# Half as many, twice as wide: preparing a projection's weights in 16 halves, and another order of banks at two stage changes of a hybrid gMLP and SSD layer

## The chip, the cores and the metric

One Trainium2 chip, one NeuronCore of it. The metric is the device time of one execution in microseconds, taken as the median of several runs. TensorE (PE) does the matmuls, VectorE (DVE), ScalarE (ACT) and GpSimd (POOL) the elementwise work, and SyncE (SP) and ScalarE issue the DMAs. [...]

## The reference

One layer of a hybrid decoder on a sequence of 1024 rows of width 1024, all float32. The lines that matter here:

```
proj = h @ w_in                                   # 11296 columns in 8 parts
y_a = spatial_gating(gelu(gm_u), gelu(gm_v), ...) * silu(gm_z)
y_b = ssd_scan(...) + xh * d_skip                 # 2048 columns
y_b = rms_norm((y_b * silu(ssm_z)) in 8 groups, ssm_norm_w)
merged = sigmoid(g_a) * (y_a @ w_proj_a) + sigmoid(g_b) * (y_b @ w_proj_b)
out = rms_norm(x + gate * (merged @ w_out), final_norm_w)
```

`h` is the normalised and modulated input; `w_proj_b` has 2048 rows and 1024 columns.

## The kernel before

**Products.** Every large product is done with a rounded high part and a remainder: an operand `t` is copied to `hi` by ScalarE (which rounds it) and VectorE computes `lo = t - hi`; the product is then the three terms hi x hi, hi x lo and lo x hi, added up in a PSUM bank of 128 x 512. The larger products are also done by a seven-product scheme of block matrices (`p1` to `p7`), which needs sums and differences of the four blocks of each operand.

**Stages in order.** Normalisation and modulation with the first gate columns (pool `ps0` of PSUM); the V block (`v_block`, lines 815 to 936), which multiplies by the V columns of `w_in`; then pairs of 128-column blocks of `w_in` (`pair`, line 536 issues the matmuls, 12 for one product, seven products for a pair); then the SSD scan, with `y_a @ w_proj_a` filled in between (`proj_a`); then `y_b @ w_proj_b`, called the second projection here (`multiply`, line 1552); then `merged @ w_out` and the last normalisation.

**Order of work.** Matmuls and all loads are pinned to program order, and with them a few copies. The other instructions of an engine are ordered by a planner ahead of time, which takes those first whose data it expects to be ready and whose place in the program is earlier. What an engine has in its list is then fixed: a copy or a store that must wait holds up all behind it on its engine. `later(d, f, ...)` puts the call `f` behind the d-th product from now; `run_tasks` is called once for each product, so a delay counts products.

**The second projection's weights.** From pair 16 on, while TensorE works on the pairs of `w_in`, the kernel forms the planes of `w_proj_b` that the seven products need and writes them to the DRAM tensors `wb_d`. A quarter `(k, j)` is 128 columns of each of four blocks: `wb_load` reads it in two DMAs on SyncE into the raw tile `wbr` (two buffers). Then `wb_parts` copies a plane to its high part on ScalarE (line 791), and one product later `wb_low` computes the remainder on VectorE (line 796) and stores both parts through ScalarE's queue. This is done for one plane (`wba`), and after the four sums on VectorE in `wb_sums` (lines 808 to 811) for two planes each in `wbb` and `wbc`. Each of the three tags has one buffer. There are 32 quarters, one for each 4.3 products; `wb_quarter` loads the next one as it begins.

**The start of the V block.** Its first four banks `vx0` to `vx3` are taken from pool `ps1`, which lies over `ps0`. The last two of `ps0`'s four accumulators are still read by the tanh of the first gate (`first_gate`, line 473, tile `sg`) when the block begins. Unit `u` is one (product, k), of 12 matmuls; units 0 and 1 run term by term over all four banks, later units bank by bank.

**The start of the second projection.** `banks` takes tiles of pool `ps3`, which lies over `ps1`, and a tag gets its bank when it is first named: `y0`, `y1`, `y2`, then `x0` to `x3`, then `y3`. p1 accumulates in the x banks. The y banks serve in p1 for four small results: `pq6_1` and `pq7_1` behind units 1 and 2, `pr6` and `pr7` behind units 3 and 4 (`rows_bank`). The last product of `proj_a` leaves two halves (`pma`) that VectorE multiplies with the gate (line 1382, tile `tha`); in the program as laid out before, they are in banks 5 and 0, and VectorE's part of them is pinned behind the operands of the first four units of p1.

Of the kernel before, what the change touches and what calls it, by code (L numbers as in the profile page):

```python
# [8 lines left out]
F32 = mybir.dt.float32  # L9
# [26 lines left out]
def hybrid_kernel(  # L36
# [739 lines left out]


    WB = {"p5": 0, "p7": 1, "p6": 2, "p3": 3, "p4": 4}
    quarters = [(k, j) for k in range(KT) for j in range(4)]
    wbr = {}  # L780

    def wb_load(i):

        k, j = quarters[i]
        wbr[i] = raw = pre.tile([P, 4, P], F32, name=f"wbr{i}", tag="wbr", bufs=2)
        for k0, t in ((k, raw[:, 0:4:3]), (k + KT, raw[:, 1:3])):
            load(t, w_proj_b[k0 * P : (k0 + 1) * P, :].rearrange("p (b j c) -> p j b c", b=2, j=4)[:, j])

    def wb_parts(i, name, at, n, t):
        hl = pre.tile([P, n, 2, P], F32R, name=f"{name}{i}", tag=name)  # L790
        A.copy(hl[:, :, 0], t)
        later(1, wb_low, i, hl, at, n, t)

    def wb_low(i, hl, at, n, t):
        k, j = quarters[i]
        V.tensor_sub(hl[:, :, 1], t, f32(hl[:, :, 0]))
        store(wb_d[k][:, at : at + n, :, j * P : (j + 1) * P], f32(hl))

    def wb_quarter(i):
        if i + 1 < len(quarters):  # L800
            wb_load(i + 1)
        wb_parts(i, "wba", 4, 1, wbr[i][:, 2:3])
        later(1, wb_sums, i)

    def wb_sums(i):
        raw = wbr.pop(i)
        a11, a12, a22, a21 = (raw[:, n] for n in range(4))
        V.tensor_add(a22, a22, a21)
        V.tensor_sub(a21, a11, a21)
        V.tensor_sub(a11, a22, a11)  # L810
        V.tensor_sub(a12, a12, a11)
        wb_parts(i, "wbb", 0, 2, raw[:, 2:4])
        wb_parts(i, "wbc", 2, 2, raw[:, 0:2])

    def v_block():

        V_OPS = (("p1", "b11", "x"), ("p5", "t1", "y"), ("p6", "t2", "x"), ("p3", "b22", "y"), ("p7", "t3", "x"),
                 ("p2", "b21", "y"), ("p4", "t4", "x"))
        units = [(nm, k) for nm, _, _ in V_OPS for k in range(4)]
        kept, wops, pair_of = {}, {}, {}  # L820
        early = 6

        def quadrant(nm, k):

            r, c = {"11": (0, 0), "21": (0, 1), "22": (4, 1), "12": (4, 0)}[nm]
            w = wt(f"av{nm}_{k}", "ws", 8, F32)
            load(w, w_in[(r + k) * P : (r + k + 1) * P, COL_V + c * 512 : COL_V + (c + 1) * 512])
            return w

        def loads(u):  # L830
            nm, k = units[u]
            live[0] += 2 if nm in ("p5", "p7") else 1
            pair_of[u] = [quadrant(q, k) for q in {"p1": ("11",), "p5": ("21", "22"), "p6": ("11",), "p3": ("12",),
                                                    "p7": ("11", "21"), "p2": ("12",), "p4": ("22",)}[nm]]

        def operands(u):
            nm, k = units[u]
            q = pair_of.pop(u)
            keep = pin if u < early else lambda i: i
            t = q[-1]  # L840
            if nm == "p5":
                keep(V.tensor_add(t, q[0], t))
                kept[k] = t
            elif nm == "p6":
                t = kept[k]
                keep(V.tensor_sub(t, t, q[0]))
            elif nm == "p3":
                t = kept.pop(k)
                keep(V.tensor_sub(t, q[0], t))
            elif nm == "p7":  # L850
                keep(V.tensor_sub(t, q[0], t))
            hi, lo = wt(f"{nm}v{k}h", "wh", 8), wt(f"{nm}v{k}l", "wl", 8)
            keep(A.copy(hi, t))
            keep(V.tensor_sub(lo, t, f32(hi)))
            wops[u] = hi, lo
            live[0] -= {"p1": 1, "p5": 1, "p6": 1, "p3": 2, "p7": 2, "p2": 1, "p4": 1}[nm]
            ahead()

        live, loaded = [0], [0]

        def ahead():
            while loaded[0] < len(units) and live[0] + (2 if units[loaded[0]][0] in ("p5", "p7") else 1) <= 8:
                loads(loaded[0])
                loaded[0] += 1

        LEAD = 3
        ahead()
        operands(0)
        operands(1)
        first_dt()  # L870
        first_gate(0)
        first_gate(1)
        open_banks()
        ps = {"x": [psum.tile([P, 512], F32, name=f"vx{j}", tag="px", bufs=2) for j in range(2)]}
        ps["x"] += [bank(f"vx{j}") for j in (2, 3)]
        res = {}

        def result(nm):
            res[nm] = [wide(f"v{nm}{i}") for i in range(2)]

        def part(nm, j):
            return res[nm][j // 2][:, j % 2 * 512 : (j % 2 + 1) * 512]

        def finished(nm, i):

            rows, c = (0, 4)[nm[2] == "2"] + 2 * i, (0, 1)[nm[1] == "2"]
            w = res[nm][i]
            A.activation(w, w, AF.Gelu_apprx_tanh)
            for j in range(2):
                V.bn_stats(bst[:, rows + j, c, :], w[:, j * 512 : (j + 1) * 512])  # L890
                store(v_d[4 * c : 4 * c + 4].rearrange("g p q -> p g q")[:, :, (rows + j) * P : (rows + j + 1) * P],
                      w[:, j * 512 : (j + 1) * 512].rearrange("p (g q) -> p g q", g=4))

        def emptied(nm):
            with tc.high_priority():
                for j in range(4):
                    b = ps["x" if nm in ("p1", "p6", "p7", "p4") else "y"][j]
                    if nm in ("p1", "p5", "p6", "p4"):
                        to = {"p1": "c11", "p5": "c22", "p6": "c12", "p4": "c21"}[nm]
                        if j == 0:  # L900
                            result(to)
                        A.copy(part(to, j), b)
                    else:
                        to = {"p3": "c12", "p7": "c22", "p2": "c11"}[nm]
                        V.tensor_add(part(to, j), part(to, j), b)
            if nm in ("p3", "p7", "p2", "p4"):
                for i in range(2):
                    later(1 + i, finished, to, i)

        for u, (nm, k) in enumerate(units):  # L910
            _, bn, pn = V_OPS[u // 4]
            if u == 4:
                ps["y"] = [bank(f"vy{j}") for j in range(4)]
            (bh, bl), (wh, wl) = (bop[bn][v][k] for v in range(2)), wops[u]
            terms = list(enumerate(((bh, wh), (bl, wh), (bh, wl))))
            for j, (n, (l, r)) in [(j, t) for t in terms for j in range(4)] if u < 2 else [(j, t) for j in range(4) for t in terms]:
                js = slice(j * P, (j + 1) * P)
                pin(PE.matmul(ps[pn][j], l[:, js], r, start=nm in ("p1", "p5", "p2") and n + k == 0,  # L918
                              stop=n == 2 and k == 3, skip_group_check=nm not in ("p1", "p5", "p2")))
            wops.pop(u)  # L920
            if u == 0:
                operands(2)
                last_split("t2")
            elif u == 1:
                operands(3)
                last_split("t3")
            elif u == 2:
                last_split("t4")
                operands(4)
            if u > 1 and u + LEAD < len(units):  # L930
                operands(u + LEAD)
            if k == 3:
                emptied(nm)
                if nm == "p3":
                    ps["y"] = [bank(f"vz{j}") for j in range(4)]
            run_tasks()
# [382 lines left out]
    for n, (name, _, _, d1, d2, g) in enumerate(todo):  # L1319
        if n == 0:  # L1320
            later(5, stats)
        if n == NPRE:
# [1 line left out]
            prepool = tc.tile_pool(name="prepool", bufs=1, side="right", reuse_waits="tile")  # L1324
            pre = prepool.__enter__()
            wb_load(0)
            for i in range(len(quarters)):
                later(2 + 43 * i // 10, wb_quarter, i)
        if n == len(jobs):
            while tasks:  # L1330
                run_tasks()
# [108 lines left out]
    room.extend(tag for k in range(KT - 2) for tag in ya_tags[k])  # L1440
    draw(left[0] - 5)

    def banks(name, c, n=4):
        return [psb.tile([P, 512], F32, name=f"{name}{j}", tag=f"b{c}{j}") for j in range(n)]

    big_r = [0]

# [218 lines left out]
    for u, (nm, k) in enumerate(units):  # L1666
        if k == 0:
            if nm == "p1":
                psy = banks("yp3", "y", 3)
                psx = banks("x", "x")  # L1670
                psy += [psb.tile([P, 512], F32, name="yp33", tag="by3")]
                rows_bank[0] = lambda name: psy[("pq6_1", "pq7_1", "pr6", "pr7").index(name)]
            elif nm in ("p5", "p2"):
                psy = banks(f"y{nm}", "y")
            ps = psy if nm in ("p2", "p5", "p3") else psx
# [206 lines left out]
```

## Time and profile before

| | us |
|---|---|
| median of 3 runs | 1404.81 (1404.6 to 1406.76) |
| the profiled execution | 1402.83 |
| its span, first to last instruction | 1401.1 |
| PE busy | 1369.7 |
| DVE busy | 1055.3 |
| ACT busy | 804.7 |
| POOL busy | 217.8 |

The mean granted clock of TensorE is 0.996. In a row of the timeline the columns are the start in us from the beginning of the span, the duration in us, the engine, the line of the kernel, the operation, `out<-in` by the program's tile names, shapes, count, and in brackets how long the engine had stood still before it and what ended that. ACTq and SPq are the DMA issues of ScalarE and SyncE. In a row for a tile stand the shortest, median and longest duration in ns and the first and last start. A row of waits has the time in total, the number of times and the longest.

### The profile page before, as it was taken

Reading aid. Unit: us, or ns where it says so; the run is one execution under the profiler, and the core shown is the slowest. Engines: PE = TensorE matmul, PEld = TensorE weight load, DVE = VectorE, ACT = ScalarE, POOL = GpSimd, SP = SyncE. Lnnn points to the kernel's source line nnn. Section 1 sums busy time; section 2 is a strip of 40 time slices with the busy share of each in tenths; the row PEclk is TensorE's granted clock in tenths of the full one; section 3 lists DMA queues with packets and bytes.
Section 4 is the critical chain, followed back from the end, with each engine's and each line's share of the span. In section 5 each row is a group of like instructions: output and inputs, shape, how many; then the busy total and the mean of one; then the engine's idle time right before and its main releaser. Section 6 shows DMA issues by size and latency. Waiting matters only on the chain.

```text
span 1401.1 us, 20579 instructions
## 1 busy us (share of the span) xinstructions
PE 1369.7 (98%) x6971; PEld 1135.3 (81%) x6971; DVE 1055.3 (75%) x1815; ACT 804.7 (57%) x1496; POOL 217.8 (16%) x208
## 2 busy tenths in 40 slices
PE   8999999999999999999999999999999999999997
PEld 7678888888888888878888888888888788888786
DVE  4776776687777889888888795398777655859976
ACT  5754656666666566455675555677676623223453
POOL 0000000000000011211000110038878750000001
PEclk9999999999999999999999999999999999999999
DMA  8775433333434777777775774598887658878913
GB/s 263 197 237 147 120 121 120 105 123 118 135 105 128 225 219 230 220 238 226 215 220 148 241 214 134 179 354 319 279 267 278 220 185 280 319 254 313 378 44 120
DMA packets 277181, 288.62 MB, mean 206 GB/s; under 512 B 15788, under 2 KB 224084, under 8 KB 277076
## 3 DMA queue, kind: packets, MB, share of 16 engines
q1 hardware_dynamic: 182420, 203.76, 45.6%
q10 hardware_dynamic: 94656, 83.54, 18.1%
q8 instruction: 55, 0.90, 0.3%
q14 instruction: 50, 0.41, 0.1%
HBM read 199.79 MB, written 87.46 MB: 205 GB/s over the span
## 4 chain that ended last, share of the span: by engine, by line
PE 78%; DVE 7%; DMA 7%; ACT 3%; issue 3%; POOL 2%; SPq 1%; ACTq 0%; DVEq 0%; POOLq 0%
PE xuz L536 6%; PE xx L536 6%; PE xcb L536 6%; PE xz L536 5%; PE xg L536 5%; PE pma L81 4%; PE yx L536 3%; PE vx L918 3%; PE x L1552 3%; PE yuz L536 3%; PE yp L1552 3%; PE ycb L536 3%; PE yz L536 3%; PE ox L1745 2%; PE yg L536 2%
## 5 line engine op out<-in xcount | busy, mean ns | idle before, releaser
L759 POOL TENSOR_TENSOR wog<-wog,gb 128x256 f32<-128x256 f32 x16 | 21.5, 1362 | 624.0 <-DMA wog<-in_w_out_dram 602.9
L1075 ACT ACTIVATE dcy<-dcy,nacs 128x128 f32<-128x128 f32 x256 | 78.7, 388 | 17.2 <-POOL dcy L1070 16.1
L1070 POOL TENSOR_SCALAR_AFFINE_SELECT dcy<-dcy 128x1024 f32<-128x1024 f32 x32 | 35.0, 1094 | 135.4 <-DMA yl<-ya_d 88.7
L990 ACT ACTIVATE ac<-ac 128x1024 f32<-128x1024 f32 x32 | 33.9, 1060 | 25.8 <-DVE ac L988 22.6
L1067 ACT ACTIVATE ea<-dcy 64x512 f32<-64x512 f32 x64 | 40.0, 626 | 12.2 <-DMA dcy<-acs_d 11.8
L81 PE MATMUL pma<-yh,wah 128*128 128x512 f32 x128 | 43.8, 423 | 0.0
L81 PE MATMUL pma<-yh,wal 128*128 128x512 f32 x128 | 43.2, 419 | 0.0
L1490 DVE SCALAR_TENSOR_TENSOR yn<-yn,par,rb 128x512 f32<-128x512 f32 x32 | 23.9, 747 | 24.8 <-DMA yn<-yb_d 24.8
L1155 DVE TENSOR_TENSOR ym<-yn,ea 128x512 f32<-128x512 f32 (+1 forms) x32 | 19.9, 622 | 29.9 <-PE yn L81 29.7
L1095 DVE TENSOR_TENSOR dcy<-dcy,pc 128x1024 f32<-128x1024 f32 x32 | 38.9, 1217 | 3.8 <-PE pc L84 2.6
L1157 POOL TENSOR_TENSOR yz<-y,sl 128x512 f32<-128x512 f32 x32 | 41.4, 1294 | 1.1
L81 PE MATMUL pma<-yl,wah 128*128 128x512 f32 x128 | 40.3, 396 | 0.0
L1156 POOL TENSOR_TENSOR y<-y,ym 128x512 f32<-128x512 f32 (+1 forms) x32 | 36.6, 1143 | 14.5 <-DVE ym L1155 14.5
L81 PE MATMUL yi<-dcy,xd 128*64 128x128 f32 x512 | 35.9, 284 | 2.9 <-DVE st L1125 2.9
L81 PEld LDWEIGHTS yn<-sl,st 128*128 128x128 f32 x224 | 30.3, 190 | 8.8 <-issue 2.7
L81 PE MATMUL yn<-sl,st 128*128 128x128 f32 x224 | 31.4, 276 | 5.4 <-DVE st L1125 5.4
L81 PE MATMUL sp<-xe,bn 128*128 128x256 f32 x112 | 33.6, 418 | 2.9 <-DVE ssq L1186 1.7
L988 DVE SCALAR_TENSOR_TENSOR ac<-c2x,cwt,ac 128x1023 f32<-128x1023 f32 (+2 forms) x24 | 31.2, 1298 | 5.7 <-ACT ac L986 5.6
L1760 POOL TENSOR_TENSOR r<-r,fnw 128x512 f32<-128x512 f32 x2 | 2.5, 1296 | 208.2 <-ACT junk L1758 208.2
L988 DVE SCALAR_TENSOR_TENSOR ac<-c2cb,cwt,ac 128x1023 f32<-128x1023 f32 (+2 forms) x24 | 31.1, 1294 | 4.8 <-ACT ac L986 4.7
L1123 POOL TENSOR_TENSOR st<-st,cd 128x256 f32<-128x256 f32 x48 | 32.5, 677 | 11.2 <-PE yn L81 7.1
L952 ACT ACTIVATE vm<-vm,vr 128x128 f32<-128x128 f32 x64 | 25.8, 483 | 14.0 <-DMA vm<-v_d 13.5
(2903 smaller groups left out, 4421.7 us busy)
## 6 DMA issues: line engine op xcount, KB each, us to landing
sl<-s_d SPq DMA_DIRECT2D x32, 768.0 KB
s_d<-ac ACTq DMA_DIRECT2D x32, 512.0 KB
dcy<-acs_d SPq DMA_DIRECT2D x32, 512.0 KB
av<-in_w_in_dram SPq DMA_DIRECT2D x36, 256.0 KB
aw<-in_ada_w_dram SPq DMA_DIRECT2D x16, 512.0 KB
wbr<-in_w_proj_b_dram SPq DMA_DIRECT2D x64, 128.0 KB
wb_d<-wbb ACTq DMA_DIRECT2D x32, 256.0 KB
wb_d<-wbc ACTq DMA_DIRECT2D x32, 256.0 KB
```

The lines of the kernel that those rows point to most:

```text
L81: pin(PE.matmul(acc, l, r, start=first, stop=last))
L536: pin(PE.matmul(ps, lw[:, k * P : (k + 1) * P], r[k], start=first and n + k == 0, stop=n == 2 and k == 3, skip_group_check=not first))
L918: pin(PE.matmul(ps[pn][j], l[:, js], r, start=nm in ("p1", "p5", "p2") and n + k == 0, stop=n == 2 and k == 3, skip_group_check=nm not in ...
L988: V.scalar_tensor_tensor(ac[:, s:], cc[:, : S - s], conv_wt[:, 3 - s, i : i + 1], ac[:, s:], op0=ALU.mult, op1=ALU.add)
L990: A.activation(ac, ac, AF.Silu)
L1067: A.activation(ea[hh * HD : (hh + 1) * HD], dcy.rearrange("p (j e) i l -> p e j (i l)", e=2)[hh * HD : (hh + 1) * HD, hh], AF.Exp)
L1070: G.affine_select(out=d8, in_=d8, compare_op=ALU.is_ge, fill=-1e30, base=0, pattern=[[0, 2 * HPG], [1, P]], channel_multiplier=-1)
L1075: A.activation(dcy[:, h, i, :], dcy[:, h, i, :], AF.Exp, bias=sub[:, i, h : h + 1])
L1095: V.tensor_tensor(d3, d3, pc[:, 0:256].unsqueeze(1).to_broadcast([P, HPG, 256]), op=ALU.mult)
L1156: G.tensor_add(y1[:, :, t0:], y1[:, :, t0:], m[:, :, t0:])
L1157: G.tensor_mul(yz, y1, sl[:, 4:6])
L1552: pin(PE.matmul(ps[j], a[:, v, js], r, start=first and n + k == 0, stop=n == 2 and k == KT - 1, skip_group_check=not first))
```

## The change

Three edits in one diff.

1. `w_proj_b` is prepared in 16 halves of 256 columns, one for each 8.6 products. The raw tile `wbr` has one buffer; its load is issued two products ahead of the half's first copy, no longer by the half before. `wbb` and `wbc` become one tag, `wbb`, of one buffer, and the second pair of planes is copied three products after the first.
2. The first two units of the V block start with two of their three terms on the first two banks only; the third and fourth banks come after that.
3. The eight banks of pool `ps3` are named in an order written out by hand: `y2, y0, x0, x1, x2, y3, x3, y1`.

```
--- before.py
+++ after.py
@@ -776,29 +776,27 @@
 
 
     WB = {"p5": 0, "p7": 1, "p6": 2, "p3": 3, "p4": 4}
-    quarters = [(k, j) for k in range(KT) for j in range(4)]
+    halves_b = [(k, j) for k in range(KT) for j in range(2)]
     wbr = {}
 
     def wb_load(i):
 
-        k, j = quarters[i]
-        wbr[i] = raw = pre.tile([P, 4, P], F32, name=f"wbr{i}", tag="wbr", bufs=2)
+        k, j = halves_b[i]
+        wbr[i] = raw = pre.tile([P, 4, 2 * P], F32, name=f"wbr{i}", tag="wbr")
         for k0, t in ((k, raw[:, 0:4:3]), (k + KT, raw[:, 1:3])):
-            load(t, w_proj_b[k0 * P : (k0 + 1) * P, :].rearrange("p (b j c) -> p j b c", b=2, j=4)[:, j])
+            load(t, w_proj_b[k0 * P : (k0 + 1) * P, :].rearrange("p (b j c) -> p j b c", b=2, j=2)[:, j])
 
     def wb_parts(i, name, at, n, t):
-        hl = pre.tile([P, n, 2, P], F32R, name=f"{name}{i}", tag=name)
+        hl = pre.tile([P, n, 2, 2 * P], F32R, name=f"{name}{at}_{i}", tag=name)
         A.copy(hl[:, :, 0], t)
         later(1, wb_low, i, hl, at, n, t)
 
     def wb_low(i, hl, at, n, t):
-        k, j = quarters[i]
+        k, j = halves_b[i]
         V.tensor_sub(hl[:, :, 1], t, f32(hl[:, :, 0]))
-        store(wb_d[k][:, at : at + n, :, j * P : (j + 1) * P], f32(hl))
+        store(wb_d[k][:, at : at + n, :, j * 2 * P : (j + 1) * 2 * P], f32(hl))
 
     def wb_quarter(i):
-        if i + 1 < len(quarters):
-            wb_load(i + 1)
         wb_parts(i, "wba", 4, 1, wbr[i][:, 2:3])
         later(1, wb_sums, i)
 
@@ -810,7 +808,7 @@
         V.tensor_sub(a11, a22, a11)
         V.tensor_sub(a12, a12, a11)
         wb_parts(i, "wbb", 0, 2, raw[:, 2:4])
-        wb_parts(i, "wbc", 2, 2, raw[:, 0:2])
+        later(3, wb_parts, i, "wbb", 2, 2, raw[:, 0:2])
 
     def v_block():
 
@@ -911,13 +909,19 @@
             _, bn, pn = V_OPS[u // 4]
             if u == 4:
                 ps["y"] = [bank(f"vy{j}") for j in range(4)]
-            (bh, bl), (wh, wl) = (bop[bn][v][k] for v in range(2)), wops[u]
-            terms = list(enumerate(((bh, wh), (bl, wh), (bh, wl))))
-            for j, (n, (l, r)) in [(j, t) for t in terms for j in range(4)] if u < 2 else [(j, t) for j in range(4) for t in terms]:
-                js = slice(j * P, (j + 1) * P)
-                pin(PE.matmul(ps[pn][j], l[:, js], r, start=nm in ("p1", "p5", "p2") and n + k == 0,
+            at = [(u, n, j) for j in range(4) for n in range(3)]
+            if u == 0:
+                ends = [(0, 2, 0), (0, 2, 1)] + [(0, n, j) for j in (2, 3) for n in range(3)]
+                at = [(i, n, j) for i in range(2) for n in range(2) for j in range(2)] + ends
+            elif u == 1:
+                at = [(1, 2, 0), (1, 2, 1)] + [(1, n, j) for j in (2, 3) for n in range(3)]
+            for i, n, j in at:
+                (bh, bl), (wh, wl) = (bop[bn][v][units[i][1]] for v in range(2)), wops[i]
+                l, r = ((bh, wh), (bl, wh), (bh, wl))[n]
+                pin(PE.matmul(ps[pn][j], l[:, j * P : (j + 1) * P], r, start=nm in ("p1", "p5", "p2") and n + units[i][1] == 0,
                               stop=n == 2 and k == 3, skip_group_check=nm not in ("p1", "p5", "p2")))
-            wops.pop(u)
+            if u:
+                wops.pop(u)
             if u == 0:
                 operands(2)
                 last_split("t2")
@@ -1324,8 +1328,10 @@
             prepool = tc.tile_pool(name="prepool", bufs=1, side="right", reuse_waits="tile")
             pre = prepool.__enter__()
             wb_load(0)
-            for i in range(len(quarters)):
-                later(2 + 43 * i // 10, wb_quarter, i)
+            for i in range(len(halves_b)):
+                if i:
+                    later(43 * i // 5, wb_load, i)
+                later(2 + 43 * i // 5, wb_quarter, i)
         if n == len(jobs):
             while tasks:
                 run_tasks()
@@ -1440,8 +1446,8 @@
     room.extend(tag for k in range(KT - 2) for tag in ya_tags[k])
     draw(left[0] - 5)
 
-    def banks(name, c, n=4):
-        return [psb.tile([P, 512], F32, name=f"{name}{j}", tag=f"b{c}{j}") for j in range(n)]
+    def banks(name, c):
+        return [psb.tile([P, 512], F32, name=f"{name}{j}", tag=f"b{c}{j}") for j in range(4)]
 
     big_r = [0]
 
@@ -1666,9 +1672,8 @@
     for u, (nm, k) in enumerate(units):
         if k == 0:
             if nm == "p1":
-                psy = banks("yp3", "y", 3)
-                psx = banks("x", "x")
-                psy += [psb.tile([P, 512], F32, name="yp33", tag="by3")]
+                first = {t: psb.tile([P, 512], F32, name=f"{t}p", tag=f"b{t}") for t in ('y2', 'y0', 'x0', 'x1', 'x2', 'y3', 'x3', 'y1')}
+                psx, psy = ([first[f"{v}{j}"] for j in range(4)] for v in "xy")
                 rows_bank[0] = lambda name: psy[("pq6_1", "pq7_1", "pr6", "pr7").index(name)]
             elif nm in ("p5", "p2"):
                 psy = banks(f"y{nm}", "y")
```

## The prediction

> **What bounds the kernel now.** I read the page first, then who waited for whom on TensorE, then the stretches around each wait in order of time.
>
> ```profile
> span 1401.1 us, 20579 instructions
> ...
> PE 1369.7 (98%) x6971; PEld 1135.3 (81%) x6971; DVE 1055.3 (75%) x1815; ACT 804.7 (57%) x1496; POOL 217.8 (16%) x208
> ```
>
> TensorE is busy for 98% of the span, so nothing that is only made cheaper on VectorE, ScalarE or the DMA queues shortens the run. Time can come only from the places where TensorE stands still. The waits of TensorE name them (in total, times, longest):
>
> ```profile
> PE vx L918 <- ACT sg L473: 1.3, 1, 1.3
> ...
> PE xz L536 <- ACT c2z L552: 1.2, 2, 0.7
> PE xg L536 <- ACT c2g L552: 1.1, 2, 0.7
> PE x L1552 <- DVE tha L1382: 1.0, 1, 1.0
> ```
>
> These four rows are what the change touches: the start of the V block (vx), the stretch in which the second projection's weights are prepared (xz, xg), and the start of the second projection (x). They add to 4.6 us of a span of 1401.1 us. The profiled execution took 1402.83 us, 1.73 us more than its span, and the median of the runs is 1404.81 us. I make the sum on the span and take the same difference off the median. A difference of 0.2%, or 2.8 us, is about what can be told from none here.
>
> **Transition one, the V block.** The chain that ended last gives TensorE's pace where nothing holds it: 48 matmuls of 512 columns in 10.88 us, so 0.2267 us each.
>
> ```profile
> 83.13 10.88 PE vy L918 x48
> ```
>
> Around the start of the block, first TensorE, then VectorE, then ScalarE (start, duration):
>
> ```profile
> 70.46 0.85 PE L918 MATMUL vx<-p1v0h,b11h 128*128 128x512 f32 x3
> 72.61 0.50 PE L918 MATMUL vx<-p1v0h,b11h 128*128 128x512 f32 x1 [1.30 <-ACT sg L473]
> 72.94 0.40 PE L918 MATMUL vx<-p1v0h,b11l 128*128 128x512 f32 x1
> ```
>
> ```profile
> 71.50 0.69 DVE L854 TENSOR_TENSOR p1v0l<-av,p1v0h 128x512 fp32r<-128x512 f32 x1
> 72.11 0.69 DVE L854 TENSOR_TENSOR p1v1l<-av,p1v1h 128x512 fp32r<-128x512 f32 x1
> ```
>
> ```profile
> 71.94 0.62 ACT L473 ACTIVATE sg<-acc 128x512 f32<-128x512 f32 x1
> ```
>
> The fourth matmul opens the fourth bank, and that bank still holds the last quarter of the first gate, which the tanh reads until 71.94 + 0.62 = 72.56. Without the wait the fifth matmul would start at 70.46 + 4 x 0.2267 = 71.37; it starts at 72.94. The loss is 1.57 us.
>
> The new order gives TensorE eight matmuls on the first two banks (two of three terms of units 0 and 1), then the third term of unit 0 there, and only then the third and fourth banks. The third bank is opened by matmul 11 (72.73) and the fourth by matmul 14, at 70.46 + 13 x 0.2267 = 73.41, 0.85 us after the tanh has ended. The order needs two operands earlier. p1v0l is first read by matmul 9, at 72.27, and is ready at 71.50 + 0.69 = 72.19. This is the next late thing, with a margin of 0.08 us; one VectorE instruction more ahead of it would give back about 0.6 us. p1v1l (ready 72.80) is read by matmul 17, at 74.09. No matmul is added, and the list of waits has no other row of the V block, so the operands behind these keep ahead of TensorE today. Bounds: 0.9 to 1.57 us saved; I take 1.57, because the rows place every operand ahead of its use. TensorE has full queues afterwards, so the whole block and what follows move up.
>
> **Transition two, proj_a to the second projection.** TensorE, then VectorE:
>
> ```profile
> 1156.42 0.39 PE L1552 MATMUL x<-p1bh,p1a 128*128 128x512 f32 x1
> ...
> 1158.93 0.50 PE L1552 MATMUL x<-p1bh,p1a 128*128 128x512 f32 x1 [0.99 <-DVE tha L1382]
> 1159.27 0.40 PE L1552 MATMUL x<-p1bl,p1a 128*128 128x512 f32 x1
> ...
> 1163.14 1.06 PE L81 MATMUL yp<-ones,sq 128*128 128x1 f32 x9
> ```
>
> ```profile
> 1156.93 0.69 DVE L1533 TENSOR_TENSOR p1a<-p1r,p1a 128x512 fp32r<-128x512 f32 x1
> ...
> 1158.20 1.28 DVE L1382 SCALAR_TENSOR_TENSOR tha<-tha,pma 128x512 f32<-128x512 f32 x2
> ```
>
> Six matmuls run on x0 and x1; the seventh opens x2, whose bank still holds half of the last product of proj_a. VectorE empties the two halves only from 1158.20, behind the operands of unit 3. The eighth matmul would start at 1156.42 + 7 x 0.2267 = 1158.01 and starts at 1159.27: 1.26 us lost. Banks are given in the order in which the code first names their tags. Before, x0 to x3 are banks 3 to 6; in the program as it is laid out the two halves lie in banks 5 and 0. After, bank 0 is y2, bank 5 is y3, and x0 to x3 are banks 2, 3, 4 and 6. y2 and y3 are first needed for the row transposes pr6 and pr7, behind units 3 and 4 of p1 and so after the yp row at 1163.14; the halves are emptied by 1158.20 + 1.28 = 1159.48. So the wait goes, with nothing late behind it: unit 3's operands end at 1157.62 and are needed at 1156.42 + 36 x 0.2267 = 1164.58. Bounds 0 (the halves lie elsewhere after the change) to 1.26; I take 1.26.
>
> Does this reach the end? The last stretch has VectorE full:
>
> ```profile
> 1230.00:1240.00 10.00, 10.00 (x46) 8.29 (x45) 2.77 (x4) 2.40 (x4) 0.00 (x0) 1.00 0.80 258
> 1300.00:1340.00 40.00, 38.66 (x170) 31.53 (x169) 40.00 (x67) 21.41 (x39) 0.00 (x0) 1.00 0.89 334
> ```
>
> ```profile
> 1328.78 0.50 PE L1745 MATMUL oy<-wlt,ma11h 128*128 128x512 f32 x1 [1.34 <-DVE wlt L1632]
> ```
>
> (The columns are stretch, length, then busy time of PE, PEld, DVE, ACT and POOL, clock, DMA share, GB/s.) From 1300 VectorE is busy all the time and TensorE waits 1.34 us for it. But between 1230 and 1240 VectorE is busy only 2.77 of 10 us, so it keeps step with TensorE there, and what it starts later moves with TensorE. I count the 1.26 us in full.
>
> **The weights.** In this stage, for all work and then for the instructions that touch the raw tile (DVE, ACT):
>
> ```profile
> 437.00:832.00 395.00, 392.69 (x1740) 323.32 (x1739) 335.56 (x623) 237.04 (x410) 34.97 (x24) 1.00 0.72 215
> ```
>
> ```profile
> 437.00:832.00 395.00, 75.68 (x224) 34.99 (x96) 1.00 0.72 215
> ```
>
> ```profile
> L808 DVE TENSOR_TENSOR wbr<-wbr x32: 276/282/833, 456.3 to 825.0; 128x128 f32<-128x128 f32 x32
> ...
> L791 ACT CAST wbb<-wbr x32: 389/406/410, 457.3 to 826.4; 128x256 fp32r<-128x256 f32 x32
> ...
> L796 DVE TENSOR_TENSOR wbb<-wbr,wbb x32: 406/416/426, 458.1 to 827.5; 128x256 fp32r<-128x256 f32 x32
> ```
>
> A doubled width costs VectorE 0.416 in place of 0.282 us (rows L808 and L796), and 512 columns 0.69 (the p1v0l row). A half then costs 5 x 0.416 + 2 x 0.69 = 3.46 us on VectorE, 55.4 us for 16, where 75.68 are spent now: 20 us less. ScalarE: 0.406 + 2 x 0.62 (the tanh row has that width) = 1.65 us, 26.3 us for 16 in place of 34.99. 64 loads become 32, 96 stores 48, with the same bytes. All of this lies beside TensorE, so by itself it is worth nothing. What counts is TensorE's loss in the stage: 395.00 - 392.69 = 2.31 us, the four waits for c2z and c2g. One of them, ScalarE then TensorE:
>
> ```profile
> 779.50 0.30 ACT L791 CAST wba<-wbr 128x128 fp32r<-128x128 f32 x1 [3.88 <-DMA wbr<-in_w_proj_b_dram]
> ...
> 785.32 0.59 ACT L552 COPY c2g<-xg 128x512 f32<-128x512 f32 x1 [0.91 <-DVE wbb L796]
> ```
>
> ```profile
> 785.96 1.20 PE L536 MATMUL xg<-t4h,p4g10h 128*128 128x512 f32 x4 [0.46 <-ACT c2g L552]
> ```
>
> ScalarE stood 3.88 us for the load of the raw tile, later 0.91 us because the store of wbb is queued in front of the copy and waits for VectorE; the copy that empties TensorE's bank was then late. Over the stage this wait for the load is the largest of ScalarE:
>
> ```profile
> ACT wba L791 <- DMA wbr<-in_w_proj_b_dram: 27.0, 15, 4.2
> ```
>
> What the change does to it has two sides. For: half as many loads, copies and stores to stand behind, and 20 us less in VectorE's queue. Against: the load is now issued two products ahead of its copy (2 x 12 x 0.2267 = 5.4 us) in place of 4.3 (11.7 us); it carries twice the bytes; and on SyncE it waits until the last reader of the one raw tile is through, with the w_in loads of the next pairs queued behind it. The last reader is issued five products after the half begins, the next load 1.6 products (4.4 us) later, so that wait should mostly be over. The second pair of planes shares the buffer of the first, so its copy on ScalarE waits for that store, issued two products earlier; behind it stand the copies that empty the banks. Best case: all four waits go, 2.31 us saved. Worst case: a wait like these four, 2.31 / 4 = 0.58 us, at each of 16 halves, 16 x 0.58 - 2.31 = 7.0 us lost. I take half of the best case, 1.2 us saved, because the stage of before is the nearest row and the work in front of the copies falls.
>
> [...]
>
> Sum: 1.57 + 1.26 + 1.2 = 4.0 us. Span 1397.1, profiled execution 1398.8, median 1400.8 us.
>
> **Rivals.**
> - All goes well: the four waits vanish too, 1.57 + 1.26 + 2.31 = 5.1 us, 1399.7 us. For it: 20 us less on VectorE. Against: the shorter lead. Chance 0.13.
> - The transitions gain and the weights cost: the load waits reach TensorE as often as now or a little more, by up to 2.8 us. 1402 to 1404.8, middle 1403. Chance 0.13.
> - The change does not do what it says at transition two: the rotating banks of proj_a are given out as they come free, and a changed order may put a half of the last product under x0 to x3 again. 1.57 + 1.2 = 2.8 us, 1402.0 us. Against: nothing near that place is changed. Chance 0.07.
> - Slower, the single raw tile: each half makes ScalarE stand for its load. TensorE feels it when the copy is more than 5.44 - 0.59 = 4.85 us late (two products less the copy). The longest wait now is 4.2 us; a lead that is 6.3 us shorter can carry it past that at every half. The stage then loses 16 times x in place of 2.31 us, against 2.83 us from the transitions. At x = 0.5 us that is 8.0 - 2.31 - 2.83 = +2.9, 1407.7 us; at 0.8 us 12.8 - 5.14 = +7.7, 1412.5 us. From 0.5 us per half it decides. For it: 15 of 32 copies wait already. Against: the planner orders ScalarE's work by when it expects the data, so the copy is likely put later. The four waits of now are 0.5 to 0.7 us each, so I price it near the lower end, 1408 us. Chance 0.22.
>
> **How the numbers follow.** Forecast 0.45, rivals 0.13, 0.13, 0.07, 0.22. Faster by over 0.2% are the forecast and the good case, 0.58; within 0.2% the second and third rivals, 0.20; slower 0.22. The forecast's own range is 1399.7 to 1402.0. The range for 8 in 10 runs from 1398.0, where VectorE's relief helps elsewhere too, to 1407.5, short of the slow rival's middle.
>
> **What would show it.** Right: no wait of vx on sg, none of x on tha, unit 2 of the V block 1.5 us earlier, TensorE's loss in the weights' stage at 1 to 2 us, VectorE's work on the raw tile near 55 us. Wrong: waits of xz, xg, xcb or xx on ScalarE's copies that add to more than 5 us, with wba or the second wbb copy standing ahead of them; or a wait of x on tha.

## The result and the profile after

The changed kernel takes 1400.2 us (median of 10 runs, 1398.12 to 1403.9), the kernel before 1406.29 us (10 runs beside it, 1404.22 to 1410.73). The ratio is 0.9958 with a 95% interval of 0.9942 to 0.9973: 5.9 us less (3.8 to 8.2). The forecast was 1400.8 us and 4.0 us less. It stood on a before of 1404.81 us, so the gains are compared here, not the times.

The profiled executions are no fair pair. The one of before took 1402.83 us, below every one of the 10 runs beside the change; the one of after took 1403.9 us, the slowest of its 10. So the spans (1401.1 and 1402.1 us) say nothing of the gain; I compare stretches between the same two matmuls instead. The head of the page of after:

```profile
span 1402.1 us, 20253 instructions
...
PE 1374.4 (98%) x6971; PEld 1139.7 (81%) x6971; DVE 1045.4 (75%) x1703; ACT 802.2 (57%) x1448; POOL 220.0 (16%) x208
```

VectorE has lost 112 instructions and 9.9 us, ScalarE 48 instructions and 2.5 us. The waits of TensorE in after (total, times, longest):

```profile
PE xx L536 <- ACT c2x L552: 2.0, 1, 2.0
PE xuz L536 <- ACT c1uz L552: 1.8, 1, 1.8
...
PE y3p L84 <- POOL ssq L1194: 0.3, 1, 0.3
...
PE oy L1750 <- DVE wlt L1638: 0.2, 1, 0.2
```

The rows of vx on sg, of x on tha and the four small ones of xz and xg are gone. A longer one of xx, one of y3p on GpSimd, and a longer one of xuz (0.27 us in before) are new.

**V block**, TensorE and then VectorE of after:

```profile
72.06 0.62 PE L921 MATMUL vx<-p1v0h,b11h 128*128 128x512 f32 x2
72.52 0.62 PE L921 MATMUL vx<-p1v0h,b11l 128*128 128x512 f32 x2
72.97 0.62 PE L921 MATMUL vx<-p1v1h,b11h 128*128 128x512 f32 x2
73.43 0.62 PE L921 MATMUL vx<-p1v1h,b11l 128*128 128x512 f32 x2
73.88 0.69 PE L921 MATMUL vx<-p1v0l,b11h 128*128 128x512 f32 x2
```

```profile
73.10 0.69 DVE L852 TENSOR_TENSOR p1v0l<-av,p1v0h 128x512 fp32r<-128x512 f32 x1
```

Eight matmuls run on two banks, and the ninth starts at 73.88, 0.09 us after its operand (73.10 + 0.69 = 73.79); the prediction had a margin of 0.08.

**Second projection**, the first matmul of p1, VectorE's part of the two halves, then the row transposes with GpSimd's power in front of the second:

```profile
1159.51 0.39 PE L1558 MATMUL x0p<-p1bh,p1a 128*128 128x512 f32 x1
...
1174.09 0.27 PE L84 MATMUL y2p<-ident,ssq 128*8 128x128 f32 x1
...
1177.40 0.27 PE L84 MATMUL y3p<-ident,ssq 128*8 128x128 f32 x1 [0.28 <-POOL ssq L1194]
```

```profile
1161.82 1.28 DVE L1388 SCALAR_TENSOR_TENSOR tha<-tha,pma 128x512 f32<-128x512 f32 x2
```

```profile
1175.71 1.64 POOL L1194 TENSOR_TENSOR ssq<-ssq,nhalf 128x8 f32<-128x8 f32 x1 [5.22 <-DVE ssq L1190]
```

TensorE no longer waits for the halves, which VectorE empties until 1163.10. It comes to the second transpose earlier, and the power ends only at 1175.71 + 1.64 = 1177.35.

**The weights' stage**: the stretch 437 to 832 of after for all work, the same for the instructions on the raw tile (DVE, ACT), then ScalarE's waits in it:

```profile
437.00:832.00 395.00, 392.95 (x1739) 324.57 (x1739) 325.62 (x512) 233.80 (x362) 36.34 (x24) 1.00 0.68 212
```

```profile
437.00:832.00 395.00, 57.97 (x111) 25.68 (x47) 1.00 0.68 212
```

```profile
ACT wba L791 <- DMA wbr<-in_w_proj_b_dram: 24.3, 11, 4.7
ACT wbb L791 <- DMA wb_d<-wbb: 23.9, 14, 3.0
```

VectorE does the raw tile in 57.97 us in place of 75.68, ScalarE in 25.68 in place of 34.99. The wait for the load is about as large as before (27.0), and beside it stands a new one: the second pair of planes waits for the store of the first, nearly every time. TensorE stood 2.05 us, in one wait:

```profile
646.23 0.41 ACT L791 CAST wba<-wbr 128x256 fp32r<-128x256 f32 x1 [4.66 <-DMA wbr<-in_w_proj_b_dram]
...
649.00 1.24 ACT L990 ACTIVATE ac<-c1x,par,cwt 128x1024 f32<-128x1024 f32 x1 [1.84 <-DVE c1x L552]
...
651.17 0.57 ACT L552 COPY c2x<-xx 128x512 f32<-128x512 f32 x1
```

```profile
651.80 1.20 PE L536 MATMUL xx<-t4h,p4x5h 128*128 128x512 f32 x4 [2.05 <-ACT c2x L552]
652.84 1.73 PE L536 MATMUL xx<-t4l,p4x5h 128*128 128x512 f32 x4
654.36 1.91 PE L536 MATMUL xx<-t4h,p4x5l 128*128 128x512 f32 x4
```

ScalarE stands 4.66 us for the load, then 1.84 us for VectorE; the copy that empties TensorE's bank is late. Then the groups of four that usually take 1.07 to 1.2 us take 1.73 and 1.91: the granted clock is 0.83 from 650 to 660 us (last section).

### The profile page after: what moved, and what is told of

Its sections match the earlier page's. It is cut to its first block, busy times and chain, and to the rows that moved or that the text cites. A ratio compares the mean times of both kernels' runs of the same rounds, so it can differ in the third digit from the quotient of the medians.

```text
span 1402.1 us, 20253 instructions
## 1 busy us (share of the span) xinstructions
PE 1374.4 (98%) x6971; PEld 1139.7 (81%) x6971; DVE 1045.4 (75%) x1703; ACT 802.2 (57%) x1448; POOL 220.0 (16%) x208
## 4 chain that ended last, share of the span: by engine, by line
PE 77%; DMA 11%; DVE 5%; ACT 2%; issue 2%; POOL 1%; SPq 1%; ACTq 0%; DVEq 0%; POOLq 0%
PE xcb L536 6%; PE xuz L536 6%; PE xz L536 6%; PE xx L536 6%; PE xg L536 5%; PE vx L921 3%; PE yz L536 3%; PE ycb L536 3%; PE yuz L536 3%; PE yx L536 3%; PE yg L536 3%; PE pma L81 3%; DMA dcy<-acs_d 2%; PE ox L1750 2%; PE oy L1750 2%
## 5 line engine op out<-in xcount | busy, mean ns | idle before, releaser
L791 ACT CAST wbb<-wbr 128x512 fp32r<-128x512 f32 x32 | 19.8, 619 | 32.6 <-DMA wb_d<-wbb 25.6
```

## Experiments

All profiles, in us between the starts of the same matmuls: "V" from the first matmul of the block to unit 2; "weights" from product p4 of column block cb4 to p1 of g12 (in before 494.02 to 878.57), with TensorE's waits in it (sum / number, from 0.15 us); "p1" the first product of the second projection; "last" from the first `oy` matmul to the end of the last matmul. "Gain" is the mean of before less the mean of the kernel over the timed runs beside each other, with its standard error.

| kernel | V | weights | waits in it | p1 | last | median | gain | ratio, 95% interval |
|---|---|---|---|---|---|---|---|---|
| before | 7.07 | 384.55 | 2.31 / 4 | 27.04 | 67.35 | | | |
| after | 5.52 | 384.82 | 2.05 / 1 | 26.22 | 66.12 | | | |
| `v_only` | 5.52 | 386.36 | 3.48 / 5 | 27.57 | 65.84 | 1405.11 | 0.9 ± 1.3 | 0.9996, 0.9975 to 1.0017 |
| `banks_only` | 7.02 | 386.37 | 2.98 / 4 | 27.35 | 67.11 | 1403.32 | 2.9 ± 0.9 | 0.998, 0.9965 to 0.9994 |
| `halves_only` | 7.05 | 385.02 | 2.43 / 1 | 27.09 | 66.15 | 1402.23 | 4.7 ± 0.9 | 0.9969, 0.9953 to 0.9984 |
| `all_again` | 5.53 | 388.42 | 5.55 / 6 | 26.44 | 65.62 | 1400.01 | 5.6 ± 0.9 | 0.9967, 0.9951 to 0.9983 |
| `quarters_kept` | 5.53 | 385.28 | 2.47 / 4 | 26.09 | 67.13 | 1402.72 | 2.9 ± 1.0 | 0.9973, 0.9953 to 0.9993 |
| `no_preparation` | 7.02 | 380.85 | 0 | 27.80 | 66.00 | 1406.15 | 0.0 ± 0.9 | 1.0, 0.998 to 1.002 |
| `load_late` | 5.54 | 388.31 | 4.49 / 8 | 27.04 | 66.07 | 1403.07 | 3.0 ± 1.1 | 0.9974, 0.9951 to 0.9998 |
| `two_waits_less` | 5.54 | 384.79 | 3.06 / 3 | 25.76 | 65.64 | 1397.89 | 7.8 ± 0.9 | 0.9949, 0.9929 to 0.9969 |
| `twice_again` | 5.51 | 384.72 | 1.97 / 1 | 25.85 | 65.62 | 1395.96 | 9.7 ± 1.1 | 0.9934, 0.9909 to 0.9959 |
| `twice_quarters` | 5.52 | 388.18 | 4.69 / 6 | 25.76 | 65.67 | 1396.84 | 8.0 ± 1.2 | 0.9944, 0.9925 to 0.9963 |
| `halves_small_ops` | 5.51 | 384.98 | 3.19 / 3 | 25.76 | 66.14 | 1397.16 | 8.1 ± 1.1 | 0.9941, 0.9921 to 0.9961 |
| `second_pair_later` | 5.51 | 384.21 | 2.66 / 2 | 25.76 | 66.13 | 1395.66 | 10.2 ± 0.9 | 0.9929, 0.9907 to 0.995 |

The first four ran beside 35 runs of before (mean 1406.05 us), the next four beside 35 others (1405.82), the last four beside 19 (1405.58); each of these series ran on a chip of its own, so kernels of different series are compared by their gains. One run of a kernel differs from another by a standard deviation of about 3 us, so a gain below 2 us is read from the traces only.

**`v_only`, `banks_only`, `halves_only`: one edit each; `all_again`: all three.** From before, only the hunks of the diff at lines 911 to 921 (V), at 1443 and 1669 (banks), or at 776 to 811 and 1327 (halves).

> Only the new order of the first two units of the V block. Theory of the prediction: 1.57 us less than before (ratio 0.9989), no wait of vx on sg, and every marker after the block earlier by 1.5 us up to the end. Rival 'given back': the c1uz copy in pair uz0 stands behind a load of vm that is tied to DMA, TensorE waits there by as much longer as it arrives earlier, so the time is within 0.3 us of before and the wait of xuz on c1uz grows from 0.27 to about 1.8 us.

> Only the new order of the banks at the second projection. Theory of the prediction: 1.26 us less (ratio 0.9991), no wait of x on tha. Rival 'given back': VectorE is full from 1300 us on, TensorE's wait of 1.34 us for wlt in the last stage grows to 2.6 us and nothing is gained.

> Only the 16 halves. Theory of the prediction: about 1.2 us less, TensorE's loss between 437 and 832 us falls from 2.31 to about 1.1 us, VectorE's work on the raw tile near 55 us. Rival 'halves are the gain': 3 us or more less, since the whole change measured 5.9 us (3.8 to 8.2) and the two transitions hold only 2.8. Rival 'single raw tile': slower than before by over 2 us.

> The whole change once more, on the same chip as its parts. If the parts act each for itself, its gain is the sum of the three; prediction 4.0 us, first measurement 5.9 us (3.8 to 8.2).

The V edit shortens its stretch by 1.55 us, and all kernels with it show 5.51 to 5.54. Its timed gain of 0.9 ± 1.3 us can show neither that gain nor its absence. In the profile of `v_only` TensorE then waits 1.91 us for c1uz, where before waited 0.27, as the rival of giving back had it; the paragraph on `two_waits_less` shows that this wait comes without the V edit too. The bank edit removes the wait of x on tha, but the profile of `banks_only` gains nothing on p1, because the next wait comes instead, on GpSimd's power (TensorE, then POOL):

```profile
1175.10 0.27 PE L84 MATMUL y3p<-ident,ssq 128*8 128x128 f32 x1 [1.43 <-POOL ssq L1190]
```

```profile
1173.40 1.64 POOL L1190 TENSOR_TENSOR ssq<-ssq,nhalf 128x8 f32<-128x8 f32 x1 [6.08 <-DVE ssq L1186]
```

The halves have the largest timed gain, 4.7 ± 0.9 us, and their trace does not show it in their own stage: 385.02 us stands against 384.55 in before, with one long wait in place of four short ones.

The timed gains of the three parts add up to 8.5 us, where `all_again` has 5.6; the error of that difference is about 2 us, so these runs do not show whether the parts add up. `all_again` is the same kernel as after, yet its profile has six waits in the weights' stage where after has one. Four of them (3.42 us) come behind a copy or a store of the preparation that stood in ScalarE's list, two (2.13 us) behind other work.

**`quarters_kept`: V and banks with the old quarters; `no_preparation`: what the preparation costs at all; `load_late`: the raw tile's load later.** The first is after without the hunks at 776 to 811 and 1327. The second is before without the preparation: one plane is stored and read in place of all of them, so its output is not the layer's. The third:

```
-                    later(43 * i // 5, wb_load, i)
+                    later(2 + 43 * i // 5, wb_load, i)
```

> The whole change but for the weights: V block and banks new, 32 quarters as before. If the halves carry 3 to 4 us, as the run of them alone says (4.4 us, 2.2 to 6.6), this one is 3 to 4 us slower than the whole change, so 1.5 to 3 us faster than before. If the prediction's sizes hold (1.57 and 1.26 us for the transitions, 1.2 for the halves), it is 2.8 us faster than before and 1.2 slower than the whole change.

> The kernel before without any preparation of the second projection's weights: two stores of other data stand for it and every unit of that projection loads one and the same plane, of the same size. It leaves the sums, copies and stores of the weights out. What is left between 437 and 832 us is TensorE without that disturbance. Theory 'halves relieve the stage': the quarters cost TensorE more in the typical run than the 2.31 us of the profile shown, so this kernel is at least 4 us faster than before. Theory of the prediction: it can be no more than 2.3 us faster, since TensorE stood only so long.

> The whole change, with the load of the raw tile issued in the same product as its first copy, two products (5.4 us) later. Slow rival: each of 16 halves then makes ScalarE stand 5 us or more for its load and TensorE loses 0.5 us and more at each, 8 us slower than the whole change. Theory 'the planner puts the copy later': within 2 us of the whole change.

`quarters_kept` and `all_again` differ by the halves: 5.6 - 2.9 = 2.7 ± 1.3 us. That lies between the 1.2 and the 3 to 4 us of the two cases expected and does not decide. Without preparation TensorE never waits in the stage:

```profile
437.00:832.00 395.00, 395.00 (x1757) 326.72 (x1756) 285.44 (x405) 220.84 (x321) 32.73 (x24) 1.00 0.47 143
```

The stretch takes 380.85 us. So the quarters of before cost TensorE 3.7 us and the halves of after 4.0, more than their waits (2.31 and 2.05): the matmuls behind a wait ran slower as well (1.20 us for the first four in place of 1.07, and up to 1.91 in after). The quarters' 3.7 us lie between what the two theories allowed (at most 2.3, at least 4).

Matmul by matmul against `no_preparation`, nearly all of the 4.0 us of after is lost at one place: the wait of xx quoted above (product p4 of column block x5) and the 16 matmuls behind it take 3.95 us more. It is 4.12 of 4.17 us in `halves_only` and all 3.86 in `twice_again`, but 1.81 of 7.57 in `all_again`, with its five further waits. All seven kernels with halves and the load in its place wait there, 1.52 to 2.43 us, after ScalarE stood 4.59 to 4.96 us for the load of that one half; the kernels with quarters and `load_late` do not wait there. A load that is issued earlier for this half alone was not tried.

The time of `no_preparation` cannot be used. Its stand-in store waits in ScalarE's list for `b11h`, ahead of a read of x, and TensorE then waits 6.42 us for x, where before waited 1.32 (ScalarE, then TensorE):

```profile
24.86 0.35 ACTq L93 DMA_DIRECT2D wb_d<-b11h  x1
25.32 1.06 ACT L367 ACTIVATE junk<-x 128x1024 f32<-128x1024 f32 x1 [6.51 <-DMA pkb<-in_conv_b_dram]
```

```profile
28.35 1.32 PE L84 MATMUL px<-ident,x 128*128 128x128 f32 x4 [6.42 <-DVE x L379]
```

(The profile names another DMA as the releaser; the store row directly in front shows what stood there.) `load_late` issues the load with the half's first copy. It loses 2.6 ± 1.4 us against all_again (5.6 - 3.0), with eight waits of together 4.49 us. The slow rival asked for a loss of 8 us. The stage itself takes 388.31 us, no more than the 388.42 of `all_again`, so the profiles do not show the loss there. That the planner and the two products of slack absorb the missing lead is likely but not shown.

**`two_waits_less`: the two waits that the traces of after showed.** It pins the copy c1uz ahead of the scalings of the mixed V (`vm`), which wait for a load, and takes the row transposes one unit later:

```
-        keep = pin if name in first_c1 and not p2r else lambda i: i
+        keep = pin if name == "uz0" or name in first_c1 and not p2r else lambda i: i
...
+        later(2, mix_norm, g, vn)
+
+    def mix_norm(g, vn):
...
-        if nm == "p1" and k in (3, 4):
-            groups[NG - 5 + k].post3()
+        if nm == "p1" and k in (4, 5):
+            groups[NG - 6 + k].post3()
```

> The whole change, and two further waits taken away: in pair uz0 the eight scalings of vm that wait for a load from DRAM come after the copy that empties TensorE's bank, and the two row transposes behind p1 come one unit later. In five of six profiles TensorE waited 1.6 to 1.9 or 0.3 us in uz0 and in three of them its clock fell right after; with the clock's loss of 1.7 us that is 0.3 to 3.5 us. Expected 1.5 to 3 us faster than the whole change, no wait of xuz on c1uz and none of y3p on ssq. Rival: the scalings come too late for the mixing product, and TensorE waits there instead.

In after, ScalarE stood for the load of `vm` while TensorE needed its bank emptied; in two_waits_less the copy comes first (ScalarE of after, then of two_waits_less, then TensorE there):

```profile
183.15 0.49 ACT L956 ACTIVATE vm<-vm,vr 128x128 f32<-128x128 f32 x1 [6.51 <-DMA vm<-v_d]
```

```profile
183.89 0.59 ACT L552 COPY c1uz<-xuz 128x512 f32<-128x512 f32 x1 [0.59 <-ACT ac L997]
```

```profile
184.53 1.20 PE L536 MATMUL xuz<-t3h,p7uz0h 128*128 128x512 f32 x4
```

All nine kernels without this change wait for c1uz. With the V edit it is 1.84 us (after), 1.91 (v_only), 2.36 (quarters_kept), 0.37 (all_again) and 0.31 (load_late); without it 0.27 (before), 1.87 (halves_only), 1.62 (banks_only) and 0.38 (no_preparation). Each time it is ScalarE's wait for the load of `vm` less 4.7 us: 4.94 and 0.27 us in before, 6.51 and 1.84 in after, 7.04 and 2.36 in quarters_kept. So it is not the V gain given back; it varies with when the load lands. The row transposes now find their data ready (POOL, then TensorE):

```profile
1167.63 1.64 POOL L1197 TENSOR_TENSOR ssq<-ssq,nhalf 128x8 f32<-128x8 f32 x1 [5.66 <-DVE ssq L1193]
```

```profile
1171.00 0.27 PE L84 MATMUL y3p<-ident,ssq 128*8 128x128 f32 x1
```

With the transposes later, p1 takes 25.76 us, 1.28 less than in before. No run has the later transposes without the bank edit. The kernel gains 2.2 ± 1.3 us on all_again (7.8 - 5.6), where 1.5 to 3 were expected, and is the fastest so far.

**`twice_again`, `twice_quarters`, `halves_small_ops`, `second_pair_later`: the halves again, with those two waits out of the way.** The first is two_waits_less once more; the second has the old quarters in it; the third splits each instruction on the raw tile; the fourth changes one delay:

```
-        A.copy(hl[:, :, 0], t)
+        for c in (slice(0, P), slice(P, 2 * P)):
+            A.copy(hl[:, :, 0, c], t[:, :, c])
```

```
-        later(3, wb_parts, i, "wbb", 2, 2, raw[:, 0:2])
+        later(4, wb_parts, i, "wbb", 2, 2, raw[:, 0:2])
```

> The kernel of two_waits_less once more, as the partner of the other three runs here. Expected 1398 us, 0.3% to 0.6% under the kernel before; TensorE waits for neither c1uz nor POOL's ssq.

> The V edit, the bank edit and the two changes of two_waits_less, but the weights prepared in 32 quarters as before. The only difference from twice_again is quarters in place of halves. Theory A (the halves are worth what the timed runs of all_again against quarters_kept and halves_only against before gave, 2.5 to 4.7 us, and it is a gain of their own): 1400.5 to 1402.5 us, and the wait of oy on wlt (line 1632 in the kernel before) of about 1.3 us is back. Theory B (the halves' gain was chance, in the stage of the weights both schemes cost TensorE the same 4.8 us): within 1 us of twice_again, about 1398 to 1399 us.

> twice_again, but every copy and every VectorE instruction on the raw tile in two of 128 columns per block, as wide as in the kernel before; loads and stores stay halves. VectorE gets its 20 us back (1055 us in place of 1045), ScalarE about 9 us more, the DMA packets stay at 247 thousand. If the halves' gain comes from the fewer instructions of VectorE and ScalarE: as slow as twice_quarters. If from the fewer and larger transfers: as fast as twice_again. If there is no gain of the halves, all three agree.

> twice_again, but the second pair of planes is copied four products after the first in place of three. Its copy waits 25.6 us in total on ScalarE for the store of the first pair, with copies that empty TensorE's banks behind it. If that wait is what the stage of the weights still loses (about 4 us more than with no preparation): that wait falls below 8 us, TensorE's waits for c2x, c2z and c2g in 437 to 850 fall by 1 to 3 us, and the time is 1 to 3 us under twice_again. Rival: the waits move to the next raw tile's load, which then has only 0.6 products of margin behind the last reader; the time stays within 1 us.

Here the halves are worth 1.7 ± 1.2 us (1395.90 against 1397.57 in the means, 0.9 in the medians). Neither theory is hit squarely: the time is nearer to B, but in the profile the quarters' stage is the longer one, 388.18 against 384.72. The wait of oy that theory A wanted back is not there. `halves_small_ops` has the mean of `twice_quarters` (1397.53 us), but with an error of 1.2 us it is not told from `twice_again` either, so fewer instructions and fewer transfers are not told apart by the time; in its profile the stage takes 384.98 us, as with the other halves. `second_pair_later` misses its own number: ScalarE's wait for the store is 24.7 us in place of 26.9, not below 8, and the time is the same within 0.5 us, as the rival said, though the wait did not move to the load (25.8 against 24.2). Why a copy placed a product later in the program waits as long was not found.

## Why the prediction was right, and where it was not

**V block: 1.57 predicted, 1.48 to 1.56 measured** (7.02 to 7.07 against 5.51 to 5.54). The margin of 0.08 us was 0.09. The gain was kept as far as the next wait, and that one is the uz0 wait, which does not depend on the edit.

**Banks: 1.26 predicted, 0.6 to 1.0 measured in after, all_again and quarters_kept** (p1 26.09 to 26.44 against 27.04 in before), and none in banks_only and load_late. (Before is itself at the low end: kernels with the old banks take 27.04 to 27.80, with a wait of x on tha of 0.99 to 1.74 us.) The wait of x on tha went as worked out. The step that failed is "with nothing late behind it". I checked unit 3's operands and the banks, not GpSimd. In before, its power and the transpose that needs it stand like this (POOL, then TensorE):

```profile
1172.40 1.65 POOL L1190 TENSOR_TENSOR ssq<-ssq,nhalf 128x8 f32<-128x8 f32 x1 [5.50 <-DVE ssq L1186]
```

```profile
1175.15 0.27 PE L84 MATMUL yp<-ident,ssq 128*8 128x128 f32 x1
```

The power ends at 1174.05, 1.10 us ahead of TensorE. A TensorE that comes 1.26 us earlier had to wait 0.16 us there at least, and more when VectorE's sums in front are later. In two_waits_less, with the transposes a unit later, no wait is left in p1 and 1.28 us are gained.

**Weights: 1.2 predicted.** Half of the best case was a guess between two bounds, and its working is wrong in one point: TensorE's loss is not 2.31 us. It is 3.7 (384.55 against 380.85 us), because a matmul that runs slowly counts as busy, as the first four behind a wait do (1.20 us in the quoted rows of xg and xx, in place of 1.07), and as the next eight in after do, where the clock is 0.83 (1.73 and 1.91 us); only the distance between two markers shows it. From start to start the first two matmuls at each of these four waits take 0.27 us more than in `no_preparation`, beyond the wait itself.

The saving of 1.2 us that the forecast put into this stage is not there in the profiles of the whole change: 384.82 us in after and 388.42 in all_again, against 384.55 in before. In after, four short waits became one long one with a clock of 0.83 in the 10 us behind it. By the prediction's own measure the stage's loss is 395.00 - 392.95 = 2.05 us, just past the 1 to 2 us that were to show it right. Only averages point the way that I said. Over the five profiles with quarters the stage takes 386.1 us, over the seven with halves and the load in its place 385.3: 0.9 us, with a spread of 384.2 to 388.4. In the last stretch the means are 66.6 and 65.9 us (here with load_late), 0.7 us more: the wait of oy on wlt is 1.22 to 1.34 us in before, banks_only and quarters_kept, and at most 0.25 in every kernel with halves, but it is also missing in v_only and twice_quarters. Together 1.6 us; with so few profiles the standard errors of the two parts are about 0.8 and 0.4 us, so neither is well clear of chance, and no mechanism behind them is shown. The timed runs give 1.7 ± 1.2, 2.7 ± 1.3 and 4.7 ± 0.9. The first two agree with 1.6; the third is too large for it, and where the rest lies is not shown. What the halves gain, and by what, stays open.

VectorE's work on the raw tile came to 57.97 us where I had 55.4, ScalarE's to 25.68 where I had 26.3.

**The slow rival** named a true mechanism: ScalarE waits for the load at 11 of 16 halves, up to 4.7 us. But in after it reached TensorE once, in all_again at four places, and never at each half. Both profiles stay on the right side of the sign of being wrong, all_again narrowly: its waits add to 5.55 us, but those behind the preparation to 3.42. My threshold of 4.85 us does not hold. At xx a wait of 4.66 us got through with 1.84 us more behind it, and elsewhere one of 3.07 us did, because the copy that empties the bank stands directly behind the `wba` copy (two_waits_less, ScalarE, then TensorE):

```profile
552.66 0.41 ACT L791 CAST wba<-wbr 128x256 fp32r<-128x256 f32 x1 [3.07 <-DMA wbr<-in_w_proj_b_dram]
552.97 0.58 ACT L552 COPY c1z<-xz 128x512 f32<-128x512 f32 x1
```

```profile
553.60 1.20 PE L536 MATMUL xz<-t2h,p6z1h 128*128 128x512 f32 x4 [0.81 <-ACT c1z L552]
```

The threshold gave every copy two products of slack, and not every copy has them. One raw tile with a lead of two products was no slower than two, by the runs of twice_again (1395.96 us) and twice_quarters (1396.84); but the tile's width differs too, and no run changes the number of buffers alone.

**The sum.** 4.0 us were predicted. The traces account for 1.5 + 0.6 to 1.0 + 1.6, so 3.7 to 4.1; the timed gain of 5.9 us has an interval of 3.8 to 8.2. The forecast's total is right within what can be measured, and in part by luck: the bank term was too large, and the term of the weights is not seen where the forecast put it. What made up for both is seen only in part, in the last stretch (66.12 us in after against 67.35).

**A version that beats both.** two_waits_less and twice_again are one kernel: 1397.89 and 1395.96 us, 7.8 and 9.7 us under before in their own series, where the whole change alone gained 5.6 and 5.9.

## What to carry to other kernels

When a wait is taken away, list every engine that delivers something to the next few microseconds of the bottleneck, the idle ones too, and write its margin beside the gain; a margin of 1.10 us under a gain of 1.26 was there to be read. A busy sum hides matmuls that run slowly (in after it shows 2.05 us lost in the weights' stage, the markers 4.0), so measure a stage between two markers. In ScalarE's list an instruction that had to wait cost what stood behind it: the scalings of `vm` (6.51 us, and then 1.84 us of TensorE, in after), the stand-in store (6.51 and 6.42 in no_preparation) and the copies of the raw tile (4.66 and 2.05 in after) all delayed a copy or a read that was ready.

## What the runs showed of the hardware

Several waits of TensorE were followed by a lower granted clock. In twice_again the wait of 1.97 us at 646.72 lies in the first of these stretches; in after the wait of 2.05 us ends at the start of the second one:

```profile
640.00:650.00 10.00, 8.03 (x29) 6.20 (x29) 9.23 (x17) 5.74 (x10) 0.00 (x0) 0.84 0.41 131
```

```profile
650.00:660.00 10.00, 8.20 (x29) 6.63 (x30) 8.97 (x13) 6.78 (x13) 0.00 (x0) 0.83 0.50 148
```

A clock of 0.83 over 10 us is by that figure 1.7 us lost, nearly as much again as the wait of 2.05. In after it is eight matmuls in a row that start 0.43 us apart in place of 0.23. The same wait in two_waits_less, only 0.08 us shorter, left the clock at 1.00:

```profile
648.27 1.20 PE L536 MATMUL xx<-t4h,p4x5h 128*128 128x512 f32 x4 [1.89 <-ACT c2x L552]
```

```profile
640.00:650.00 10.00, 8.11 (x37) 6.38 (x36) 9.09 (x19) 4.68 (x8) 0.00 (x0) 1.00 0.45 155
```

In the stages of the products a fall stood behind the waits of 1.84 us (after, 0.94 from 180 to 190 us), 1.91 (v_only, where the first four matmuls took 1.38 us in place of 1.20), 1.97, 2.05 and 2.43 (halves_only, 0.83 from 650 to 660 us); none stood behind 1.52 (all_again), 1.62 (banks_only), 1.73 (halves_small_ops) and 1.89, with 1.00 in the windows of all four. So the length of the wait alone did not decide between 1.84 and 1.89 us. Nor did it in the SSD scan: a fall followed one of 1.44 us (all_again, where four matmuls of sp took 2.01 us; behind 1.68 us in banks_only they took 1.10), and none one of 2.14 (before, 1.00 from 1020 to 1030 us). What decides it is not shown. One wait of 2.05 us cost about as much as four of 0.46 to 0.68 us: 4.0 us in after, 3.7 in before.

Between p1 of g12 and the second projection, where no edit has an instruction, the stretch takes 272.5 us in banks_only and 278.9 in load_late. The runs of one kernel differ by up to 16 us (before: 1398.13 to 1414.45), more than any edit here. Over 70 of its runs the mean time was 1407.7 us at a mean clock of 0.994 (9 runs) and 1400.6 at 0.999 (2 runs). With 12 runs of each, two kernels 2 us apart cannot be told apart by the time alone.
